# Weight splits held back by a count of VectorE's queue, and a quarter of the down projection moved between two block products

## The chip, the cores and the metric

The kernel is one program on one core of a Trainium2 chip. The metric is the device time of one execution in microseconds. Three executions of the kernel before took 2178.36, 2178.17 and 2172.22 us; the median is 2178.17 us.

## The reference, cut to what matters

Two transformer stacks run one after the other on 256 tokens of 1024 channels, all in fp32: four layers (a mixer, then a SwiGLU feed-forward), then two blocks of feed-forward, mixer, feed-forward. So there are eight feed-forward layers, four `ffn` and four `ffn_a`/`ffn_b`, all with a hidden width of 2816. The change touches only how these are scheduled, and how weights are prepared for every stage:

```python
def _swiglu(xn, w_gate, w_up, w_down):
    return (jax.nn.silu(xn @ w_gate) * (xn @ w_up)) @ w_down
...
f = _swiglu(_rms(x, g[2]), ffn_w_gate[i], ffn_w_up[i], ffn_w_down[i])
x = x + _rms(f, g[3])
```

## The kernel before, in words

**fp32 by three products.** Each fp32 operand is split into a high and a low half of type fp32r. `mm3` (line 270) multiplies high by high, high by low and low by high, three matmuls of 512 columns (lines 273, 274, 275), and then calls `tick` (line 242). One tick is thus the unit in which the program lays out its work.

**How a weight gets ready.** A weight piece of 1 MB is loaded by SyncE (line 149, in `load_step`) into one of 19 large SBUF buffers (`r8`). A unit of work is one piece, or the sum of two. `split_step` (line 189) takes the next unit in an order fixed in advance (`plan_ffn`, line 443) and splits one half of it, 128x1024: ScalarE casts it to the high half (line 220), and VectorE later subtracts to get the low half (line 184, in `flush`, which keeps one subtraction pending). If the unit is a sum, VectorE first adds the two pieces in two instructions (line 176, `pre_add`). A unit is not split further ahead than `ahead` units past the one in use, nor when `limit` units are live or fewer than two buffers are free. `need` (line 228) forces a unit's split if it has not been issued when a product wants it.

**Tasks.** Each `tick` calls `split_step` once, then steps the tasks whose time has come. A task is a generator; `spawn(gen, delay)` makes it run `delay` ticks later (at once if 0), `join` runs it on the spot. Every engine executes its instructions in the order in which the program issued them, so this order decides which instruction stands behind which.

**The feed-forward.** The hidden width is cut in chunks of 512 columns, c = 0 to 4, and one of 256. Chunks 2 and 4 (`SUMS`) are computed by `seven` (line 568), which forms the four 128x512 blocks (gate and up, for each token half) from seven block products instead of eight, in PSUM banks X, Y and Z. Each product is four ticks. Between the products stand four quarters of the down projection of the chunk before, also four ticks each: `down(c-1, h, (q,))` is token half h with weight unit q, and the unit's buffers are given back after h = 1. The order in `seven` is

- products b11 (X), b21 (Z), t1 (Y), t2 (X),
- `down(c-1,0,(0,))`, `down(c-1,1,(0,))`,
- products b22 (Y), t3 (X),
- `down(c-1,0,(1,))`, `down(c-1,1,(1,))`,
- product t4 (X).

Between products on the same bank the bank is read: X by ScalarE `copy("1")` before t2 goes on top of it, Y by `copy("5")` before b22, X by `copy("2")` before t3 (all line 587), and X by VectorE in `up1` (line 605) before t4. `gate0` (line 591) and its Silu (line 593, ScalarE) and `up0` (lines 597 and 599) are the other evacuations. The units are prepared in the order b11, b21, t1, t2, the first down unit, b22, t3, the second down unit, t4. Two `seven` in each of eight layers make 16.

Of the kernel before, what the change touches and what calls it, by code (L numbers as in the profile page):

```python
# [50 lines left out]
class Core:  # L51
    def __init__(self, ctx, tc, I, out):
        self.tc, self.nc, self.I, self.out = tc, tc.nc, I, out
        P = lambda name, **kw: ctx.enter_context(tc.tile_pool(name=name, bufs=1, **kw))
        sb = P("sb")
        self.sb = sb
        self.r8 = Slots(sb, "r8_", 19, W8, F32R)
        self.r2 = Slots(sb, "r2_", 6, 512, F32R)
        self.f2 = Slots(sb, "f2_", 10, 512, F32)
        self.gn = Slots(sb, "gn_", 2, D, F32)  # L60
        self.ps = Slots(P("ps", space=PSUM), "ps_", 8, 512, F32)
        self.dram = P("dram", space=DRAM)
        self.small_pool = sb
        self.n_small = 0
        self.later = []
        self.ticks = 0
        self.tasks = []
        self.pieces = []
        self.n_dma = self.n_split = 0
        self.sub = 0  # L70
        self.cur, self.ahead = -1, 2
        self.limit = 6
        self.live = 0
        self.raw, self.hl, self.xt = {}, {}, {}
        self.units, self.lows = [], deque()
        self.begun, self.waiting, self.n_low = set(), 0, 0
        self.uses, self.summed = [], set()
        self.z = {}
        self.raw_max = 3
        self.spare = 2  # L80
        self.reserve = 0
        self.hold = 0
        self.rr, self.nr = {}, {}
        self.pre_gains = deque()
        self.gains, self.gq = deque(), deque()
# [55 lines left out]
    def load_step(self, most=10 ** 9):  # L141
        while self.n_dma < most and self.n_dma < len(self.pieces) and len(self.r8.free) > self.spare + self.reserve and self.waiting < self.raw_max:
# [9 lines left out]
            self.waiting += 1  # L152
            self.n_dma += 1

    def used(self, i):
        self.uses[i] -= 1
        if not self.uses[i]:
            self.r8.put(self.raw.pop(i))
# [6 lines left out]
    def pre_add(self, i):  # L165

        src, first = self.units[i]
        if first is None or i in self.summed:
            return True
        if src not in self.raw or first not in self.raw or any(self.units[j][0] == src for j in range(self.n_low, i)):  # L170
            return False
        self.begin(src)
        self.begin(first)
        a, b = (self.view(self.raw[n], src) for n in (src, first))
        for sl in (slice(0, 2), slice(2, 4)):
            self.nc.vector.tensor_tensor(out=a[:, sl], in0=a[:, sl], in1=b[:, sl], op=ALU.add)  # L176
        self.used(first)
        self.summed.add(i)
        return True

    def flush(self, keep=0):
        while len(self.lows) > keep:
            lo, raw, hi, eng, i, last = self.lows.popleft()
            eng.tensor_tensor(out=lo, in0=raw, in1=hi.bitcast(F32), op=ALU.subtract)  # L184
            if last:
                self.n_low = i + 1
                self.used(self.units[i][0])

    def split_step(self, force=False, eng=None):
        i = self.n_split  # L190
        if i >= len(self.units):
            self.flush()
            return False
        src, first = self.units[i]
        if self.sub == 0:
            if first is not None and i not in self.summed:
                self.flush()
            if not force:
                for j in range(i + 1, min(i + 2, len(self.units))):
                    if self.units[j][1] is not None and j not in self.summed:  # L200
                        self.pre_add(j)
                        break
            self.load_step()
            if not force and (self.hold or i > self.cur + self.ahead or self.live >= self.limit or len(self.r8.free) < 2 + self.reserve):
                self.flush()
                self.load_step()
                return False
            if src not in self.raw or not self.pre_add(i):
                self.flush()
                return False  # L210
            if len(self.r8.free) < 2:
                self.flush()
            self.hl[i] = (self.r8.get(), self.r8.get())
            self.live += 1
            self.begin(src)
        hi, lo = (self.view(t, src) for t in self.hl[i])
        k = hi.shape[1]
        sl = slice(0, k // 2) if self.sub == 0 else slice(k // 2, k)
        raw = self.view(self.raw[src], src)[:, sl]
        self.nc.scalar.copy(out=hi[:, sl], in_=raw)  # L220
        self.lows.append((lo[:, sl], raw, hi[:, sl], eng or self.nc.vector, i, self.sub == 1))
        self.flush(1)
        self.n_split += self.sub
        self.sub ^= 1
        self.load_step()
        return True
# [52 lines left out]
    def split(self, hi, lo, src, scale=None):  # L279

        if scale is None:
            self.nc.scalar.copy(out=hi, in_=src)  # L282
            self.nc.vector.tensor_tensor(out=lo, in0=src, in1=hi.bitcast(F32), op=ALU.subtract)  # L283
        else:
            self.nc.scalar.activation(out=hi, in_=src, func=ACTF.Copy, scale=scale)
            self.nc.vector.scalar_tensor_tensor(out=lo, in0=src, scalar=scale, in1=hi.bitcast(F32), op0=ALU.mult, op1=ALU.subtract)
# [100 lines left out]
    def x_sums(self):  # L387

        tt, stt = self.nc.vector.tensor_tensor, self.nc.vector.scalar_tensor_tensor
        while len(self.r8.free) < 2:  # L390
            yield 1
        self.xs = (self.r8.get(), self.r8.get())
        self.reserve = 0
        z = self.z

        def put(j, t):
            self.split(self.xs[0][:, j * 512:(j + 1) * 512], self.xs[1][:, j * 512:(j + 1) * 512], t)

        tt(out=z[1, 1], in0=z[1, 1], in1=z[1, 0], op=ALU.subtract)
        tt(out=z[1, 0], in0=z[0, 0], in1=z[1, 0], op=ALU.subtract)  # L400
        put(0, z[1, 1])
        yield 6
        stt(out=z[0, 0], in0=z[1, 1], scalar=-1.0, in1=z[0, 0], op0=ALU.mult, op1=ALU.subtract)
        put(3, z[1, 0])
        yield 6
        stt(out=z[0, 1], in0=z[0, 0], scalar=-1.0, in1=z[0, 1], op0=ALU.mult, op1=ALU.subtract)
        put(1, z[0, 0])
        yield 6
        put(2, z[0, 1])
        self.f2.put(*z.values())  # L410
        z.clear()
        yield
# [69 lines left out]
    def ffn(self, plan, half, nxt):  # L482
# [51 lines left out]
        def both(c):  # L534
# [21 lines left out]

            def up(h, b):
                nc.vector.scalar_tensor_tensor(out=s[h], in0=b, scalar=rr[h], in1=s[h], op0=ALU.mult, op1=ALU.mult)  # L558
                self.ps.put(b)
                hidden(s[h], c, h, 512, 11)  # L560
                yield

            for q, use in enumerate((gate, up)):
                half_chunk(q, use)
                for h in range(2):
                    down(c - 1, h, (q,))

        def seven(c):
# [20 lines left out]

            def gate0():  # L590
                nc.vector.tensor_tensor(out=f["1"], in0=Z, in1=f["1"], op=ALU.add)
                self.ps.put(Z)
                nc.scalar.activation(out=f["1"], in_=f["1"], func=ACTF.Silu, scale=rr[0])
                yield

            def up0():
                nc.vector.tensor_tensor(out=f["2"], in0=Y, in1=f["2"], op=ALU.add)
                self.ps.put(Y)
                nc.vector.scalar_tensor_tensor(out=f["2"], in0=f["2"], scalar=self.nr[0], in1=f["1"], op0=ALU.mult, op1=ALU.mult)
                self.f2.put(f["1"])  # L600
                hidden(f["2"], c, 0, 512, 12)
                yield

            def up1():
                nc.vector.tensor_tensor(out=f["5"], in0=X, in1=f["5"], op=ALU.add)  # L605
                yield

            def gate1():
                g = self.f2.get()
                nc.scalar.activation(out=g, in_=X, func=ACTF.Silu, scale=rr[1])  # L610
                self.ps.put(X)
                nc.vector.scalar_tensor_tensor(out=f["5"], in0=f["5"], scalar=self.nr[1], in1=g, op0=ALU.mult, op1=ALU.mult)
                self.f2.put(g)
                hidden(f["5"], c, 1, 512, 12)
                yield
# [9 lines left out]
            product(X, "t2", "s2")  # L625
            e4 = self.spawn(copy("2", X), 2)
            down(c - 1, 0, (0,))
            down(c - 1, 1, (0,))
            self.join(e2, e3)
            product(Y, "b22", "s4")  # L630
            self.join(e4)
            e5 = self.spawn(up0(), 2)
            product(X, "t3", "s3")
            e6 = self.spawn(up1(), 1)
            down(c - 1, 0, (1,))
            down(c - 1, 1, (1,))
            self.join(e5, e6)
# [1074 lines left out]
```

## Time and profile before

| what | value |
|---|---|
| median of three executions | 2178.17 us |
| the profiled execution: time / span | 2174.96 / 2172.8 us |
| TensorE (PE) busy | 2108.3 us, 97% of the span |
| VectorE (DVE) busy | 1562.1 us, 72% |
| ScalarE (ACT) busy | 1210.7 us, 56% |
| mean granted TensorE clock | 0.995 of full speed |

The span runs from the first to the last instruction. A busy share is an average over all stages; what a change in one stage can bring is read from the idle time of PE in that stage and from what ended it.

### The profile page before, as it was taken

The page shows a single profiled execution, that of the slowest core. Times are in us where ns is not written, and L with a number is a line of the kernel's source. Part 1 is how long each engine was busy: PE and PEld are TensorE (multiplying, and loading weights), DVE is VectorE, ACT ScalarE, POOL GpSimd, SP SyncE. Part 2 cuts the span into 40 slices and gives each one's busy share as a digit, 9 for nine tenths or more (in the row PEclk, how much of TensorE's full clock was granted, in tenths as well). Part 3 has the DMA queues.
Part 4 walks back from the last instruction along what each step waited for, and adds up shares of the span by engine and source line. Part 5 has one row for each costly group of instructions (what it writes and reads, how often), then busy time and mean ns, then how long its engine had stood idle before and what let it go on. Part 6 is the DMA issues. An engine that isn't in the chain of part 4 may idle for free. (4 is left out here: it accounts for less than half of the span.)

```text
span 2172.8 us, 25010 instructions
## 1 busy us (share of the span) xinstructions
PE 2108.3 (97%) x9653; PEld 1691.3 (78%) x9653; DVE 1562.1 (72%) x2016; ACT 1210.7 (56%) x1742; POOL 77.9 (4%) x130
## 2 busy tenths in 40 slices
PE   9999989999999999999999999999999999999998
PEld 6877767777888778887788777878778787787786
DVE  6677668876577776688767765787778776479774
ACT  5555446555665555555555546774556545667543
POOL 1000000000010000000000002010000001000000
PEclk9999999999999999999999999999999999999999
DMA  8546454646444555545554564345554545344442
GB/s 294 194 162 228 150 184 143 225 156 204 157 139 174 200 198 179 194 165 194 184 193 144 171 221 164 123 142 175 201 210 168 201 151 203 123 168 163 166 155 97
DMA packets 175622, 383.74 MB, mean 177 GB/s; under 512 B 10428, under 2 KB 29116, under 8 KB 175504
## 3 DMA queue, kind: packets, MB, share of 16 engines
q1 hardware_dynamic: 172592, 372.04, 49.4%
q0 software_dynamic: 2624, 9.58, 1.3%
q8 instruction: 76, 1.25, 0.2%
q10 hardware_dynamic: 288, 0.52, 0.1%
q14 instruction: 42, 0.34, 0.0%
HBM read 380.28 MB, written 1.84 MB: 176 GB/s over the span
## 5 line engine op out<-in xcount | busy, mean ns | idle before, releaser
L273 PE MATMUL ps<-r,r 128*128 128x512 f32 (+2 forms) x2752 | 1109.0, 403 | 44.7 <-DVE f L605 37.5
L274 PE MATMUL ps<-r,r 128*128 128x512 f32 (+2 forms) x2752 | 1083.9, 394 | 4.9 <-DVE r L184 3.4
L275 PE MATMUL ps<-r,r 128*128 128x512 f32 (+2 forms) x2752 | 1085.5, 394 | 0.5 <-DVE r L283 0.3
L184 DVE TENSOR_TENSOR r<-r,r 128x1024 fp32r<-128x1024 f32 (+1 forms) x797 | 935.8, 1217 | 200.9 <-ACT r L220 197.4
L220 ACT CAST r<-r 128x1024 fp32r<-128x1024 f32 x798 | 791.7, 1043 | 412.7 <-DVE r L176 185.9
L273 PEld LDWEIGHTS ps<-r,r 128*128 128x128 f32 (+1 forms) x2752 | 518.0, 188 | 171.1 <-DVE f L605 44.4
L275 PEld LDWEIGHTS ps<-r,r 128*128 128x128 f32 (+1 forms) x2752 | 516.8, 188 | 127.0 <-DVE r L283 7.3
L274 PEld LDWEIGHTS ps<-r,r 128*128 128x128 f32 (+1 forms) x2752 | 518.0, 188 | 119.7 <-DVE r L184 8.3
L176 DVE TENSOR_TENSOR r<-r,r 128x1024 f32<-128x1024 f32 x128 | 150.9, 1220 | 54.1 <-DMA r<-in_ffn_w_up_dram 27.6
L282 ACT CAST r<-ps 128x512 fp32r<-128x512 f32 (+1 forms) x108 | 59.9, 555 | 169.0 <-PE ps L498 160.7
L283 DVE TENSOR_TENSOR r<-ps,r 128x512 fp32r<-128x512 f32 (+1 forms) x108 | 69.6, 648 | 104.3 <-ACT r L282 104.3
L558 DVE SCALAR_TENSOR_TENSOR f<-ps,rr,f 128x512 f32<-128x512 f32 x32 | 23.9, 748 | 71.8 <-PE ps L275 71.8
L302 POOL TENSOR_TENSOR st<-st,c_mhalf 128x1 f32<-128x1 f32 x28 | 16.0, 570 | 1600.2 <-DVE st L301 1599.8
L282 ACT CAST r<-f 128x512 fp32r<-128x512 f32 x84 | 51.5, 619 | 37.9 <-DVE f L366 22.1
L306 ACT ACTIVATE c_junk<-x 128x512 bf16<-128x512 f32 x56 | 35.3, 631 | 54.6 <-DVE x L339 53.7
L283 DVE TENSOR_TENSOR r<-f,r 128x512 fp32r<-128x512 f32 x84 | 57.5, 709 | 3.6 <-ACT r L282 1.5
L498 PEld LDWEIGHTS ps<-c_ident,f 128*128 128x128 f32 x352 | 45.7, 144 | 13.6 <-issue 0.8
L498 PE MATMUL ps<-c_ident,f 128*128 128x128 f32 x352 | 55.7, 278 | 0.0
L366 DVE TENSOR_TENSOR f<-ps,c_pre 128x512 f32<-128x512 f32 x52 | 33.7, 687 | 23.1 <-PE ps L292 22.5
L339 DVE SCALAR_TENSOR_TENSOR x<-f,st,x 128x512 f32<-128x512 f32 x56 | 39.6, 749 | 2.6 <-POOL st L302 0.9
L331 DVE TENSOR_TENSOR f<-ps,gn 128x512 f32<-128x512 f32 x52 | 35.5, 683 | 6.1 <-ACT c_junk L306 6.1
L530 DVE SCALAR_TENSOR_TENSOR f<-ps,rr,f 128x512 f32<-128x512 f32 (+1 forms) x32 | 19.7, 615 | 27.4 <-ACT f L529 27.3
(193 smaller groups left out, 947.7 us busy)
## 6 DMA issues: line engine op xcount, KB each, us to landing
r<-in_ffn_w_in_dram SPq DMA_DIRECT2D x80, 1024.0 KB, 5.2
r<-in_ffn_w_down_dram SPq DMA_DIRECT2D x44, 1024.0 KB, 5.0
r<-in_ffn_w_out_dram SPq DMA_DIRECT2D x44, 1024.0 KB, 5.1
r<-in_ffn_w_gate_dram SPq DMA_DIRECT2D x40, 1024.0 KB, 5.1
r<-in_ffn_w_up_dram SPq DMA_DIRECT2D x40, 1024.0 KB, 5.2
r<-in_mix_w_in_dram SPq DMA_DIRECT2D x28, 1024.0 KB, 5.1
r<-in_conv_w_in_dram SPq DMA_DIRECT2D x22, 1024.0 KB, 5.5
r<-in_attn_w_qkv_dram SPq DMA_DIRECT2D x12, 1024.0 KB, 5.4
```

What stands on the lines that cost most here:

```text
L176: self.nc.vector.tensor_tensor(out=a[:, sl], in0=a[:, sl], in1=b[:, sl], op=ALU.add)
L184: eng.tensor_tensor(out=lo, in0=raw, in1=hi.bitcast(F32), op=ALU.subtract)
L220: self.nc.scalar.copy(out=hi[:, sl], in_=raw)
L273: mm(out=out, lhsT=x[0], rhs=w[0], start=first, stop=False, skip_group_check=more)
L274: mm(out=out, lhsT=x[0], rhs=w[1], start=False, stop=False, skip_group_check=more)
L275: mm(out=out, lhsT=x[1], rhs=w[0], start=False, stop=last, skip_group_check=more)
L282: self.nc.scalar.copy(out=hi, in_=src)
L283: self.nc.vector.tensor_tensor(out=lo, in0=src, in1=hi.bitcast(F32), op=ALU.subtract)
L306: self.nc.scalar.activation(out=self.junk[:, 0:src.shape[-1]], in_=src, func=ACTF.Square, scale=scale, accum_out=acc)
L331: mul = lambda n: nc.vector.tensor_tensor(out=mg[n], in0=src[n], in1=g[:, n * 512:(n + 1) * 512], op=ALU.mult)
L339: nc.vector.scalar_tensor_tensor(out=xs, in0=mg[n], scalar=r, in1=xs, op0=ALU.mult, op1=ALU.add)
L498: nc.tensor.transpose(out=b[:, j * 128:(j + 1) * 128], in_=s[:, j * 128:(j + 1) * 128], identity=self.ident)
```

## The change

It has two parts. A count, `vector_until`, notes in ticks until when VectorE would be occupied by what has been issued: each noted instruction of `cols` columns adds (cols + 60)/640 ticks. `split_step`, unless forced, returns at once, before it loads, adds, casts or flushes anything, while the count is more than 1.5 ticks ahead. And in `seven`, `down(c-1,1,(0,))` moves from before b22 to after t3, and `up1` is spawned with no delay, so that it is issued straight behind t3 instead of one tick into the next quarter. The count is noted at lines 176, 184, 283, 399 to 406, 558, 591, 597, 599, 605 and 612; the diff is cut to three of these.

```diff
+        self.vector_until = 0.0
...
+    def vector(self, cols):
+
+        self.vector_until = max(self.vector_until, self.ticks) + (cols + 60) / 640
+
...
             self.nc.vector.tensor_tensor(out=a[:, sl], in0=a[:, sl], in1=b[:, sl], op=ALU.add)
+            self.vector(1024)
...
             eng.tensor_tensor(out=lo, in0=raw, in1=hi.bitcast(F32), op=ALU.subtract)
+            self.vector(1024)
...
             self.flush()
+            return False
+        if not force and self.vector_until > self.ticks + 1.5:
             return False
         src, first = self.units[i]
...
                 nc.vector.tensor_tensor(out=f["5"], in0=X, in1=f["5"], op=ALU.add)
+                self.vector(512)
                 yield
...
             down(c - 1, 0, (0,))
-            down(c - 1, 1, (0,))
             self.join(e2, e3)
             product(Y, "b22", "s4")
             self.join(e4)
             e5 = self.spawn(up0(), 2)
             product(X, "t3", "s3")
-            e6 = self.spawn(up1(), 1)
+            e6 = self.spawn(up1(), 0)
+            down(c - 1, 1, (0,))
             down(c - 1, 0, (1,))
             down(c - 1, 1, (1,))
             self.join(e5, e6)
```

## Rows read from the trace of the kernel before

**Rows 1.** The page, busy time of each engine.
```profile
PE 2108.3 (97%) x9653; PEld 1691.3 (78%) x9653; DVE 1562.1 (72%) x2016; ACT 1210.7 (56%) x1742; POOL 77.9 (4%) x130
```
**Rows 2.** Waits of PE: line waited for, us in total, times, longest.
```profile
PE ps L273 <- DVE f L605: 37.5, 16, 7.2
...
PE ps L273 <- ACT f L587: 2.6, 2, 2.3
```
**Rows 3.** Timeline, one `seven`, PE: start us, us, [idle before <-releaser].
```profile
781.35 0.19 PEld L273 LDWEIGHTS ps<-r,r 128*128 128x128 f32 x1 [0.50 <-ACT f L587]
...
792.66 0.50 PE L273 MATMUL ps<-r,r 128*128 128x512 f32 x1 [2.65 <-DVE f L605]
```
**Rows 4.** Timeline, the same `seven`, ScalarE.
```profile
772.27 0.72 ACT L593 ACTIVATE f<-f,rr 128x512 f32<-128x512 f32 x1 [2.78 <-DVE f L591]
774.54 2.95 ACT L220 CAST r<-r 128x1024 fp32r<-128x1024 f32 x3 [1.54 <-DVE r L176]
777.39 0.58 ACT L587 COPY f<-ps 128x512 f32<-128x512 f32 x1
777.87 2.95 ACT L220 CAST r<-r 128x1024 fp32r<-128x1024 f32 x3
780.72 0.58 ACT L587 COPY f<-ps 128x512 f32<-128x512 f32 x1
...
787.17 2.00 ACT L220 CAST r<-r 128x1024 fp32r<-128x1024 f32 x2 [1.98 <-DMA r<-in_ffn_w_up_dram]
```
**Rows 5.** Timeline, the same `seven`, VectorE.
```profile
768.16 3.48 DVE L184 TENSOR_TENSOR r<-r,r 128x1024 fp32r<-128x1024 f32 x3
771.56 0.68 DVE L591 TENSOR_TENSOR f<-ps,f 128x512 f32<-128x512 f32 x1
772.16 2.35 DVE L176 TENSOR_TENSOR r<-r,r 128x1024 f32<-128x1024 f32 x2
774.43 8.21 DVE L184 TENSOR_TENSOR r<-r,r 128x1024 fp32r<-128x1024 f32 x7
...
788.25 1.23 DVE L184 TENSOR_TENSOR r<-r,r 128x1024 fp32r<-128x1024 f32 x1 [1.61 <-ACT r L220]
789.40 0.68 DVE L597 TENSOR_TENSOR f<-ps,f 128x512 f32<-128x512 f32 x1
...
790.79 1.22 DVE L184 TENSOR_TENSOR r<-r,r 128x1024 fp32r<-128x1024 f32 x1
791.92 0.69 DVE L605 TENSOR_TENSOR f<-ps,f 128x512 f32<-128x512 f32 x1
```
**Rows 6.** The chain that ended last: start us, us from one matmul to the next.
```profile
2142.57 0.23 PE ps L273
```
**Rows 7.** Groups by line: busy us, mean ns of one | idle before.
```profile
L274 PE MATMUL ps<-r,r 128*128 128x512 f32 (+2 forms) x2752 | 1083.9, 394 | 4.9 <-DVE r L184 3.4
```
**Rows 8.** Timeline, PE: the first matmul of t4 in three other `seven`.
```profile
274.92 0.80 PE L273 MATMUL ps<-r,r 128*128 128x512 f32 x1 [7.18 <-DVE f L605]
...
1011.16 0.50 PE L273 MATMUL ps<-r,r 128*128 128x512 f32 x1 [2.32 <-DVE f L605]
...
1271.99 0.79 PE L273 MATMUL ps<-r,r 128*128 128x512 f32 x1 [2.57 <-DVE f L605]
```
**Rows 9.** Windows: us, busy of PE, PEld, DVE, ACT, POOL, clock, DMA, GB/s.
```profile
274.90:278.65 3.75, 3.73 (x11) 3.06 (x12) 2.23 (x2) 0.00 (x0) 0.00 (x0) 0.50 0.88 280
794.07:797.48 3.41, 3.41 (x12) 2.75 (x11) 3.12 (x4) 2.28 (x3) 0.00 (x0) 0.50 1.00 362
1012.50:1015.90 3.40, 3.40 (x12) 2.73 (x11) 3.40 (x4) 1.06 (x2) 0.00 (x0) 0.50 0.96 355
1271.93:1275.30 3.37, 3.31 (x9) 2.62 (x10) 2.74 (x4) 1.61 (x3) 0.00 (x0) 0.50 0.83 270
```
**Rows 10.** DMA issues: KB each, median us from issue to landing.
```profile
r<-in_ffn_w_down_dram SPq DMA_DIRECT2D x44, 1024.0 KB, 5.0
```

More of the change, by code (lines that the diff above doesn't have):

```diff
@@ L400, in x_sums @@
         tt(out=z[1, 0], in0=z[0, 0], in1=z[1, 0], op=ALU.subtract)
+        self.vector(1024)
         put(0, z[1, 1])
@@ L403, in x_sums @@
         stt(out=z[0, 0], in0=z[1, 1], scalar=-1.0, in1=z[0, 0], op0=ALU.mult, op1=ALU.subtract)
+        self.vector(512)
         put(3, z[1, 0])
@@ L406, in x_sums @@
         stt(out=z[0, 1], in0=z[0, 0], scalar=-1.0, in1=z[0, 1], op0=ALU.mult, op1=ALU.subtract)
+        self.vector(512)
         put(1, z[0, 0])
@@ L558, in up @@
                 nc.vector.scalar_tensor_tensor(out=s[h], in0=b, scalar=rr[h], in1=s[h], op0=ALU.mult, op1=ALU.mult)
+                self.vector(512)
                 self.ps.put(b)
@@ L591, in gate0 @@
                 nc.vector.tensor_tensor(out=f["1"], in0=Z, in1=f["1"], op=ALU.add)
+                self.vector(512)
                 self.ps.put(Z)
@@ L597, in up0 @@
                 nc.vector.tensor_tensor(out=f["2"], in0=Y, in1=f["2"], op=ALU.add)
+                self.vector(512)
                 self.ps.put(Y)
                 nc.vector.scalar_tensor_tensor(out=f["2"], in0=f["2"], scalar=self.nr[0], in1=f["1"], op0=ALU.mult, op1=ALU.mult)
+                self.vector(512)
                 self.f2.put(f["1"])
@@ L605, in up1 @@
                 nc.vector.tensor_tensor(out=f["5"], in0=X, in1=f["5"], op=ALU.add)
+                self.vector(512)
                 yield
@@ L612, in gate1 @@
                 nc.vector.scalar_tensor_tensor(out=f["5"], in0=f["5"], scalar=self.nr[1], in1=g, op0=ALU.mult, op1=ALU.mult)
+                self.vector(512)
                 self.f2.put(g)
```

## The prediction, made before the change was run

> **What bounds the kernel now.** I read the busy shares first: TensorE is busy in 97% of the span, VectorE in 72%, ScalarE in 56% [rows 1]. The reader is to see that some 64 us without a matmul are all that scheduling can win. Next the list of what PE waited for [rows 2]: 37.5 of these 64 us are one wait, 16 times, once in each `seven`: t4's first matmul waits for line 605, `up1`, which reads bank X. The copies' wait named beside it is 2.6 us, twice.
>
> Why is `up1` late? The timelines of one `seven` tell [rows 3 to 5]. A matmul follows the last in 0.23 us [rows 6], so a tick of three is 0.70 us. t3 starts at 781.35 and ends 2.8 us later, at 784.15; X could be read from then on. Two quarters of the down projection (5.6 us) cover the read, to 789.75; t4 starts at 792.66. VectorE reads X only at 791.92. Just ahead of it stand `up0` and two low halves of weights, and the first of these, at 788.25, came after an idle 1.61 us for a cast that itself waited for a load [rows 4, 5]. These weights are wanted only after t4. So VectorE is not short of speed here: its queue holds work for later, issued early, in front of work for now.
>
> ScalarE shows the same. `copy("5")` may run when t1 ends (8 + 4 ticks after the first product starts; with t3 at tick 28 = 781.35, tick 0 is 761.75 and this is 770.15), but runs at 777.39, behind three casts that waited for VectorE's adds; `copy("2")` at 780.72 stands behind three more [rows 4].
>
> **What the stall costs.** The profile's 37.5 us count idle from a matmul's modelled end, 0.39 us after its start [rows 7], where the next could start after 0.23. Each stall therefore hides 0.16 us more: 37.5 + 16 x 0.16 = 40 us. There is a second price. After the wait in this `seven` and in three others [rows 3, 8] a stretch is granted half clock, 1.2 instead of 2.4 GHz, for 3.41, 3.75, 3.40 and 3.37 us [rows 9]; PE stood idle before all four, and I read the idle time as the reason. At half speed half of the time is lost: 13.9 / 2 = 7 us. I take both as gone if the wait goes: 47 us.
>
> **The moved quarter.** It is 12 matmuls, four ticks, 2.8 us. It issues no load, but its end returns a down unit's two buffers eight ticks (5.6 us) later. Behind t3, cover for `up1` grows from 8 to 12 ticks, 8.4 us. In front of b22 cover shrinks by 2.8 us: b22 would start at 775.75 and t3 at 778.55 without waits. With the queues as they are, `copy("5")` ends at 777.97, b22 waits 2.2 us and ends at 780.8, and t3 waits 0.5 us more for `copy("2")`, done at 781.30. So the move alone would lose 16 x 2.7 = 43 us of the 47. Everything hangs on what the hold does to the two queues.
>
> **The hold.** A low half is noted as 1084/640 = 1.69 ticks, 1.18 us. The trace has three in 3.48 and seven in 8.21 us, 1.16 to 1.17 each [rows 5], so the count runs true while VectorE waits for nothing. I counted this `seven` by hand under the new rule, in ticks from its first product, with the buffers that become free: a cast adds nothing, its low half is noted with the next cast, and a step goes only if the count is at most 1.5 past the tick. The count stands at 9.7 after the evacuation at tick 4; b22's casts are held to ticks 9 and 10 and its low halves end at 11.7 and 14.3 with `gate0` (12.6) between them; t3's casts go at 13 and 14, its first low half ends at 16.0; the two adds of t4 and t3's second low half end at 21.1; then nothing is issued until tick 20. The second down unit and t4 follow at 20 to 25; `up0` (26) ends at 29.6 and `up1` (28) at 30.5.
>
> - b22 starts at tick 20: its weights are 5.7 ticks early. `copy("5")` is issued at 14 behind t3's two casts alone (2.00 us by the pair in rows 4): Silu to about 13.6, casts to 16.6, copy to 17.4. In time by 2.6 ticks, 1.8 us.
> - t3 starts at 24 and wants its second half at 26: 8 and 4.9 ticks early (3.4 us for the nearer). `copy("2")` is issued at 18 behind one cast: done by 20, 4 ticks early.
> - t4 starts at 40: `up1` is done 9.5 ticks, 6.6 us, before. Ahead of it stand only low halves of t4 and the down unit; the first of a later unit, and so the one whose load was late, comes behind it, at tick 30.
>
> So the evacuations' wait goes and the weights still arrive. Total work on each engine is unchanged. VectorE's later work moves into the chunk behind, where `both` wants 12 low halves in 48 ticks. A load is issued with the hold up to four ticks later, but its start is set by the buffer: the second down piece is asked for at tick 9, lands 5.0 us (7 ticks) later [rows 10], and is wanted at tick 32. Elsewhere one unit alone never trips the hold (1.69 - 1 = 0.69, then 3.39 - 2 = 1.39 ticks ahead), and units are issued several ticks before their product, so I cost the hold outside `seven` at nothing; each that came late would cost up to a low half, 1.2 us [rows 5].
>
> What I charge: the wait of b22 or t3 for a copy, seen twice before [rows 2], has less room in the first `seven`, where loads start late. Bounds are nothing and 43 us (above); nearest is the count's margin of 1.8 us, so I take 0.2 us for each of the 16, 3 us. Sum: 2174.96 - 47 + 3 = 2131 against the profiled execution's time. That execution lies 3.2 us below the median shown, so I forecast between the two, **2133 us**; its own range is 2124 to 2144.
>
> **A rule against it.** t4's gap comes back in all 16, 2.3 us in the mean [rows 2]. The Trainium skill (Perfetto Trace Analysis, "Optimization Strategy") says that a gap repeating on the engine that should be saturated can mean that SBUF has too few buffers for the next tile. By that rule holding two buffers 5.6 us longer makes it worse; the trace agrees in part, since a load was waited for. It is the second rival below, and is priced there from rows.
>
> **The rivals.**
>
> - *The waits move to the copies.* If other casts stay ahead of `copy("5")` and `copy("2")`, or the hold does not bite before tick 14, PE waits 2.7 us a `seven` in place of t4's: 2175 - 47 + 43 = 2171, no change to speak of. For it: three casts stand in front of each copy now. Against: the count leaves two and one. Decides: `copy("5")` later than tick 20. Chance 0.08.
> - *Buffers, and loads with them.* If the units behind t4 get in front of `up1` again, or the later buffers delay what `down` wants next, each `seven` keeps about the 1.6 us that VectorE idled for a cast [rows 5]: 16 x 1.6 = 26 us, and half of the clock's 7 with it: 2131 + 29 = 2160. Against: the count puts these low halves two ticks behind `up1`. Chance 0.12.
> - *Held too long (slower).* If the hold keeps t3's unit back until its product asks, `need` forces it: two adds, a cast and a low half before the first matmul, 2 x 1.17 + 1.0 + 1.22 = 4.6 us [rows 4, 5], 16 times 74: 2175 - 47 + 74 = 2202. It decides where t3's second low half ends over 5 ticks later than counted, and is slower than before from 47/16 = 2.9 us beyond that. For it: held steps also flush and load nothing. Against: 3.4 us of room, and a count that matches the rows. Chance 0.06.
> - Forecast 0.74.
>
> **How the numbers follow.** What a measurement of this kernel can tell from no change is about 0.3%, 6.5 us. Faster: the forecast and the second rival, and a quarter of the first, 0.88. Same: most of the first, 0.06. Slower: 0.06. The range reaches from all named waits gone (2131 - 3 - 3.4 - 2.6 = 2122; the 3.4 is what lines 274 waited for low halves, rows 7) up to the second rival, 2160; outside are the first and the third, 0.14, and some misses.
>
> **What would show it.** In the profile after: PE's wait for `up1` near nothing; `up1` right behind t3, with about five low halves between t4's adds and `up0`, where rows 5 show eight and more; fewer than three casts before each copy; half-clock stretches behind t4 gone; no new line of PE waiting over 5 us. I am wrong if line 587 or 184 takes the place of the wait, or if forced splits appear in `seven`.

## The result, and the profile after

The changed kernel takes 2119.04 us (median; 2118.69 to 2120.63), the kernel before 2178.24 us beside it. The ratio is 0.9736 with a 95% interval of 0.9719 to 0.9754: 2.6% faster. The direction is as forecast, but the time lies 14 us under the 2133 forecast, 5 us under the forecast's own range (from 2124) and 3 us under the lower end of the wide one (2122). The profiled execution took 2119.03 us, 55.9 less than that of before, with a span of 2116.5 and a mean granted clock of 0.999 (0.995 before).

The page's busy times answer to [rows 1]; the number of instructions is the same, and PE's share rises to 99%:

```profile
PE 2090.4 (99%) x9653; PEld 1688.8 (80%) x9653; DVE 1559.2 (74%) x2016; ACT 1211.7 (57%) x1742; POOL 76.9 (4%) x130
```

Of the 56 us gained, PE's idle time is 38 (span less busy: 64.5 before, 26.1 after) and its busy time the other 18. The prediction's sentence that the 64 us without a matmul are all that scheduling can win was thus no bound: busy time holds delays too, as shown below.

The waits of PE answer to [rows 2]. `up1` (now line 622) is in the list no more; the costliest of what is left is a tenth of it, and for a copy (now line 601) PE waits once. The third line, the low half of the hidden tile (the product of gate and up that `down` multiplies), has grown from 0.3 us:

```profile
PE ps L283 <- DVE r L190: 3.9, 7, 1.3
PE ps L302 <- DVE x L349: 3.7, 3, 2.0
PE ps L284 <- DVE r L292: 3.0, 4, 1.2
...
PE ps L282 <- ACT f L601: 1.1, 1, 1.1
```

The timelines of the same `seven`, ScalarE and VectorE, answer to [rows 4, 5]. Here b22 starts at 754.50, t3 at 757.30 and t4 at 768.88:

```profile
750.41 2.00 ACT L229 CAST r<-r 128x1024 fp32r<-128x1024 f32 x2 [0.40 <-DVE r L190]
752.32 0.58 ACT L601 COPY f<-ps 128x512 f32<-128x512 f32 x1
752.79 1.05 ACT L229 CAST r<-r 128x1024 fp32r<-128x1024 f32 x1
753.75 0.58 ACT L601 COPY f<-ps 128x512 f32<-128x512 f32 x1
```

```profile
752.64 2.35 DVE L181 TENSOR_TENSOR r<-r,r 128x1024 f32<-128x1024 f32 x2
754.91 5.76 DVE L190 TENSOR_TENSOR r<-r,r 128x1024 fp32r<-128x1024 f32 x5
760.59 0.69 DVE L612 TENSOR_TENSOR f<-ps,f 128x512 f32<-128x512 f32 x1
761.31 0.75 DVE L615 SCALAR_TENSOR_TENSOR f<-f,rr,f 128x512 f32<-128x512 f32 x1
761.98 0.68 DVE L622 TENSOR_TENSOR f<-ps,f 128x512 f32<-128x512 f32 x1
```

Two casts and one cast stand in front of the copies where there were three and three, and five low halves stand between t4's adds and `up0` where rows 5 show eight and more. The copies end 1.6 and 3.0 us before their product, `up1` 6.2 us before t4.

### The profile page after: what moved, and what is told of

Read it like the earlier page. It is cut to its first block, busy times and chain, and to the rows that moved or that the text cites. A ratio compares the mean times of both kernels' runs of the same rounds, so it can differ in the third digit from the quotient of the medians.

```text
span 2116.5 us, 24989 instructions
## 1 busy us (share of the span) xinstructions
PE 2090.4 (99%) x9653; PEld 1688.8 (80%) x9653; DVE 1559.2 (74%) x2016; ACT 1211.7 (57%) x1742; POOL 76.9 (4%) x130
## 5 line engine op out<-in xcount | busy, mean ns | idle before, releaser
L316 ACT ACTIVATE c_junk<-ps 128x512 bf16<-128x512 f32 x52 | 31.0, 597 | 17.0 <-PE ps L284 16.2
```

Of the source, the lines that this page charges most:

```text
L316: self.nc.scalar.activation(out=self.junk[:, 0:src.shape[-1]], in_=src, func=ACTF.Square, scale=scale, accum_out=acc)
```

## The experiments

All of them stand beside runs of the kernel before on the same chip. Runs 1 to 4, 5 to 8, 9 to 12 and 13 to 16 are four groups, each on a chip of its own; only the groups of runs 5 and 13 have the change itself beside the others, so elsewhere a difference of a few us to the change is less sure. Line numbers of the variants differ by a few.

| run | median us | ratio to before | 95% interval |
|---|---|---|---|
| the change | 2119.04 | 0.9736 | 0.9719 to 0.9754 |
| 1 move alone | 2175.56 | 1.0000 | 0.9984 to 1.0015 |
| 2 hold alone | 2124.43 | 0.9767 | 0.9743 to 0.9792 |
| 3 hold in `seven` only | 2123.33 | 0.9767 | 0.9742 to 0.9791 |
| 4 `up1` late | 2168.27 | 0.9972 | 0.9955 to 0.9988 |
| 5 the change again | 2119.59 | 0.9748 | 0.9727 to 0.9769 |
| 6 hold, `up1` at once | 2124.16 | 0.9766 | 0.9748 to 0.9783 |
| 7 quiet before `up1` | 2156.81 | 0.9918 | 0.9893 to 0.9943 |
| 8 count a third larger | 2393.84 | 1.1007 | 1.0974 to 1.1040 |
| 9 hold up to b22 | 2161.37 | 0.9938 | 0.9919 to 0.9957 |
| 10 limit 3.0 | 2120.61 | 0.9750 | 0.9734 to 0.9766 |
| 11 limit 0.7 | 2116.82 | 0.9731 | 0.9716 to 0.9746 |
| 12 count a quarter larger | 2127.19 | 0.9779 | 0.9763 to 0.9794 |
| 13 the change, a third time | 2118.68 | 0.9747 | 0.9732 to 0.9761 |
| 14 hold alone again | 2123.31 | 0.9770 | 0.9755 to 0.9785 |
| 15 limit 0.7 again | 2115.85 | 0.9736 | 0.9722 to 0.9751 |
| 16 hold alone, limit 0.7 | 2116.82 | 0.9739 | 0.9722 to 0.9757 |

**1. The move without the hold.**

```diff
-        if not force and self.vector_until > self.ticks + 1.5:
+        if not force and self.vector_until > self.ticks + 1e9:
```

> The quarter moved and up1 undelayed, but no hold (the limit of 1.5 ticks is set out of reach). Theory (the prediction's): without the hold the copies still run behind three casts each, so b22 and t3 wait 2.7 us a seven in place of up1: 16 x 2.7 = 43 us given back of the 47, about 2171 us, and PE's waits name line 587's copy (line 601 here) with some 30 to 45 us. Rival: the move itself brings most of the gain, since cover for up1 grows by 2.8 us where the stall was 2.3: 2125 to 2140 us, and the copies' wait stays under 10 us.

Measured 2175.56 us, no change. The list of PE's waits names the copies:

```profile
PE ps L282 <- ACT f L601: 42.1, 26, 5.3
```

ScalarE's timeline shows them where [rows 4] had them, behind three casts each:

```profile
773.15 2.94 ACT L229 CAST r<-r 128x1024 fp32r<-128x1024 f32 x3 [1.54 <-DVE r L181]
776.00 0.57 ACT L601 COPY f<-ps 128x512 f32<-128x512 f32 x1
776.47 2.95 ACT L229 CAST r<-r 128x1024 fp32r<-128x1024 f32 x3
779.32 0.58 ACT L601 COPY f<-ps 128x512 f32<-128x512 f32 x1
```

The wait for `up1` is gone and an equal one has taken its place, 42.1 us of idle time where 43 were worked out (46 by the starts of matmuls, the measure of the table further down). The moved quarter alone brings nothing.

**2. The hold without the move.**

```diff
             down(c - 1, 0, (0,))
+            down(c - 1, 1, (0,))
             self.join(e2, e3)
...
-            e6 = self.spawn(up1(), 0)
-            down(c - 1, 1, (0,))
+            e6 = self.spawn(up1(), 1)
```

> The hold with the old order of quarters and up1 one tick late as before. Theory: the order of VectorE's queue is what made up1 late, so the hold alone takes the 16 waits away: up1 is issued at tick 33 with a count of about 35.6 against t4 at 40, and both copies have 2.8 us more room than after the change: 2115 to 2125 us, no wait for up1 over 3 us in total. Rival: cover of 12 ticks is needed, and up1 still waits behind two low halves of later units (issued at ticks 29 and 30): 0.7 to 1.6 us a seven remain, 2130 to 2145 us.

Measured 2124.43 us, within the theory's range: nearly all of the gain comes from the hold. Of the waits for `up1` one of 0.3 us is left.

**3. The hold inside `seven` only.**

```diff
-        if not force and self.vector_until > self.ticks + 1.5:
+        if not force and self.in_seven and self.vector_until > self.ticks + 1.5:
...
                 self.join(self.st)
+                self.in_seven = True
                 seven(c)
+                self.in_seven = False
```

> The change, with the hold in force only inside seven; everywhere else splits are issued as before the change. Theory (the hold outside seven costs and brings nothing): 2116 to 2122 us, the same as the change within 0.2%. Rival: part of the 12 us beyond the forecast comes from the hold in other stages: 2125 to 2131 us.

Measured 2123.33 us, between the two: its runs (2122.41 to 2126.36) lie 1.6 to 7.7 us over those of the change (2118.69 to 2120.78 in the result and run 5), so the hold elsewhere brings perhaps 4 us. In its list of PE's waits the low half of the hidden tile stands with 6.5 us in 8 waits, against 3.0 in 4 after the change. It was not run beside the change, and the intervals against before overlap: a hint, not more.

**4. `up1` put back late.**

```diff
-            e6 = self.spawn(up1(), 0)
+            e6 = self.spawn(up1(), 99)
```

`join` then issues it just ahead of t4.

> The change, with up1 issued only right before t4, behind a low half of a later unit; copies and weights keep the order of the change. This puts back the one wait and nothing else. Theory: PE waits for up1 about 2.0 to 2.5 us in each seven, 32 to 40 us, and half-clock stretches come back behind some of these waits (0 to 7 us): 2150 to 2166 us. What it falls short of the kernel before (2178) is then the part of the gain that is not up1: the copies and their like, some 10 us. Rival: all of the gain hangs on up1 and the clock: 2170 to 2180 us.

Measured 2168.27 us, above the theory's range by 2 us and under the rival's. PE waits again, and the mean granted clock is back at 0.994 in the profiled execution (0.990 to 0.995 over all ten; before beside it 0.989 to 0.997):

```profile
PE ps L282 <- DVE f L622: 39.5, 16, 3.7
```

```profile
core 0: 2164.6 us, clock 0.994
```

This one wait with its clock is worth about 2168.3 - 2119.3 = 49 us, where 2119.3 is the mean of the result and run 5. The other 8 us of the gain (2176.1 - 2168.3; 2.6 to 9.8 by the interval) are something else.

**5 and 6. The change again, and the hold with `up1` undelayed in the old order.** Run 6 is run 2 with `spawn(up1(), 0)`.

> The changed kernel once more, beside the three others of this call. Both theories: 2117 to 2122 us.

> The hold, the old order of the quarters, and up1 issued without delay right behind t3. Theory: with the hold up1 is in time anyway, so this tick is worth nothing: the same as the hold alone, 2121 to 2126 us, and what is left to the change (2119) is what the moved quarter brings by issuing up0 four ticks earlier, and with it the transposes of the hidden tile whose low half PE waited for 5.8 us with the hold alone and 3.0 us after the change. Rival: the missing tick of up1 is the difference, 2117 to 2120 us.

Measured 2119.59 and 2124.16 us, side by side, with runs that do not overlap (2119.15 to 2120.78, 2122.24 to 2124.84). Issuing `up1` one tick earlier is worth nothing that shows (2124.16 with it, 2124.43 without it in run 2); the rival falls.

**7. Quiet from b22 to `up1`, no count.** The kernel before with this:

```diff
+        if not force and self.quiet:
+            return False
         src, first = self.units[i]
...
             self.join(e2, e3)
+            self.quiet = True
             product(Y, "b22", "s4")
...
                 nc.vector.tensor_tensor(out=f["5"], in0=X, in1=f["5"], op=ALU.add)
+                self.quiet = False
```

> The kernel before (no count, quarters in the old order, up1 one tick late) with one thing added: from b22 on no split is issued until up1 is issued. So the casts of the units behind t4, and their low halves, go behind up1; the queue up to b22 is as long as before. Theory: these few low halves, with the load they wait for, are the whole stall: up1 runs 3 us or more before t4, 40 us and 7 us of clock come back, the copies' small waits stay (2 to 6 us): 2124 to 2132 us. Rival: the long queue that VectorE carries since t1 (busy without a gap to 782.64 in the seven of rows 5) still makes up1 late: a stall of 0.5 to 1.5 us stays in most, 2140 to 2155 us.

Measured 2156.81 us, 2 us above the rival's range and far from the theory's. `up1` is in time and its wait is gone, as the theory says; but PE has a new one, for the high half of the hidden tile (`split`, here line 285), which `down` wants next:

```profile
PE ps L276 <- ACT r L285: 22.4, 10, 8.4
```

ScalarE's timeline shows why. The casts of later units, which now stand behind `up1`, still wait for their loads, and the hidden tile's cast stands behind them:

```profile
785.68 1.99 ACT L223 CAST r<-r 128x1024 fp32r<-128x1024 f32 x2 [0.99 <-DMA r<-in_ffn_w_up_dram]
789.38 1.99 ACT L223 CAST r<-r 128x1024 fp32r<-128x1024 f32 x2 [1.70 <-DMA r<-in_ffn_w_down_dram]
791.27 0.58 ACT L285 CAST r<-ps 128x512 fp32r<-128x512 f32 x1
```

Half clock costs this run 12 us of extra time, by the measure of the table further down, where it cost the kernel before 8. So my price for this edit was wrong: to move the late splits behind one reader hands their wait to the next.

**8 and 12. The count a third and a quarter larger.** 480 and 512 in place of 640 columns a tick.

> The change with every note a third larger (480 columns a tick in place of 640), so that the count no longer runs with VectorE but ahead of it. The third rival's case (held too long): about 125 units are then issued only when their product asks, each at about 2.3 us for cast and low half, sums 4.6 us: 290 to 450 us more than the change, 2400 to 2570 us, with PE waiting for line 190. Against it, if VectorE still has its slack and the forced splits hide behind other work: under 2200 us.

> The change with every note a quarter larger (512 columns a tick). No more forced splits than in the change beyond one unit, but units of seven are issued only 2 to 5 ticks ahead of their product, where the change has 8 and more. Theory: this is the edge on the way to the slow case: PE waits for line 190 in most seven, 0 to 1.5 us each: 2120 to 2145 us. Rival: the loss starts only where splits are forced: 2117 to 2122 us.

Measured 2393.84 us, 10% slower than before, just under what was worked out, and 2127.19 us, within the theory's range. PE's waits of the former, which make up 176 of the 275 us that it takes more than the change (some 75 us of the rest are extra time at half clock, by the measure of the table further down; the mean granted clock is 0.957):

```profile
PE ps L282 <- ACT r L229: 111.8, 54, 6.6
PE ps L283 <- DVE r L190: 64.1, 82, 2.5
```

and the first of the latter:

```profile
PE ps L283 <- DVE r L190: 13.0, 13, 3.6
```

The slow rival is real. In the change the count is at 640 columns a tick; at 512 the weights begin to come late, and at 480 the kernel falls over the edge.

**9. The hold only up to b22, in the old order.** `early` is true from the first product of `seven` to b22.

```diff
-        if not force and self.vector_until > self.ticks + 1.5:
+        if not force and self.early and self.vector_until > self.ticks + 1.5:
```

> The old order of quarters, up1 one tick late, and the hold in force only from the start of seven up to b22. From b22 on splits are issued freely, so the same two low halves of the unit behind t4 stand around up0 in front of up1 as in the kernel before. Theory as mended by the run that was quiet before up1: those low halves were late because their load was, and the load because its buffer was freed late by VectorE's long queue; with the early hold the load starts 3 us sooner, so they no longer wait and up1 is in time though it stands behind them: 2121 to 2130 us, ScalarE's waits for loads well under the 119 us of before. Rival: it is the order alone, so up1 is late again by 1 us or more in most seven: 2140 us and up.

Measured 2161.37 us: the mended theory falls, the rival's range holds. PE waits for `up1` (here line 623) again, if less, and for the hidden tile:

```profile
PE ps L283 <- DVE f L623: 20.6, 15, 3.6
PE ps L283 <- ACT r L292: 11.5, 8, 3.4
```

VectorE's timeline of the `seven` whose t4 starts at 720.35 shows that here no late load was needed for it:

```profile
707.91 9.17 DVE L191 TENSOR_TENSOR r<-r,r 128x1024 fp32r<-128x1024 f32 x8
717.00 0.68 DVE L613 TENSOR_TENSOR f<-ps,f 128x512 f32<-128x512 f32 x1
...
718.39 1.22 DVE L191 TENSOR_TENSOR r<-r,r 128x1024 fp32r<-128x1024 f32 x1
719.52 0.68 DVE L623 TENSOR_TENSOR f<-ps,f 128x512 f32<-128x512 f32 x1
```

VectorE does not stand idle ahead of `up1`; eight low halves in front of `up0` and one behind it are enough to make `up1` late. Neither a shorter queue ahead of b22 (run 9) nor a free way from b22 to `up1` (run 7) was enough; of the versions run here, those whose hold lasts through `seven` take the waits away.

**10, 11 and 13 to 16. The limit, and the moved quarter once more.** 3.0 and 0.7 ticks in place of 1.5.

> The change with 3.0 ticks in place of 1.5 as the limit of the hold. Theory: about one more half is let into each queue; up1 keeps its room, copy 5 runs a tick later but before tick 20: 2117 to 2126 us. Rival: the margin of copy 5 (2.2 ticks measured) is used up and the copies wait again: 2130 us and up.

> The change with 0.7 ticks as the limit. Theory: splits go one at a time, weights still 5 ticks early in issue: 2116 to 2124 us, the same as the change. Rival: t3's second half is late and PE waits for line 190 some 10 to 30 us: 2130 to 2150 us.

> The changed kernel, five rounds beside the next three. 2118 to 2121 us.

> The hold with the old order of quarters once more. Theory (the moved quarter adds to the hold, since up0 and with it the hidden tile's split come four ticks earlier): 4 to 5.5 us above the change, 2122 to 2126 us, with an interval that excludes no difference. Rival: the difference between calls was drift: within 1.5 us of the change.

> The limit of 0.7 ticks, beside the change. Theory (a shorter queue goes on paying, since casts are issued later and find their loads landed): 2 to 3.5 us under the change, 2115 to 2118 us. Rival: same as the change within 1 us.

> The old order of quarters with the limit of 0.7. Theory: only one low half of a later unit stands before up1 and none waits for a load; the moved quarter still brings its 4 to 5 us: 2119 to 2124 us. Rival: with the shorter queue the move is worth nothing: 2115 to 2118 us.

The limit of 3.0 measured 2120.61 us, that of 0.7 2116.82. In runs 13 to 16, side by side, the change took 2118.68 us (2118.24 to 2119.62), the hold alone 2123.31 (2122.59 to 2125.75): the moved quarter brings 4.6 us on top of the hold. The medians at 0.7 are 2115.85 us with it and 2116.82 without, runs overlapping: there it brings nothing that can be told. The median at the limit of 0.7 is 2.8 us under that of the change, but the runs only just do not touch (2115.72 to 2118.16 against 2118.24 to 2119.62); it is the lowest median here.

Where at least a part of the 4.6 us is shows in what the weight loads of PE waited for. The low half of the hidden tile, line 292, in the change, the hold alone, the limit of 0.7 and that without the move (runs 13 to 16), one line of each view:

```profile
PEld ps L284 <- DVE r L292: 9.2, 18, 1.5
```

```profile
PEld ps L284 <- DVE r L292: 15.8, 27, 1.9
```

```profile
PEld ps L284 <- DVE r L292: 4.1, 13, 0.4
```

```profile
PEld ps L284 <- DVE r L292: 4.3, 14, 0.4
```

15.8 - 9.2 = 6.6 us go with the moved quarter at 1.5, and nothing at 0.7. Not all of a weight load's wait is lost to the matmuls: in PE's own list the same wait is 2.8 and 4.9 us (runs 13 and 14). With the quarter moved `up0` is issued four ticks earlier, and the hidden tile's transposes and split with it; that the split finds VectorE free anyway with the shorter limit is my reading of the last two lines, not a test.

## Why the prediction was right, and where its size was wrong

**The bound and the stall.** Right. `up1` was late through the order of VectorE's queue, not through its speed: busy time is the same (1559.2 us after, 1562.1 before) and the wait is gone. The price was right too: the table below has 40.0 + 6.6 us for the 47 worked out from idle, pace and clock, and run 4, which puts back such a wait alone, is 49 us slower. The 7 us of the clock were for the four stretches behind `up1`, which cost 6.4; a fifth stretch at half clock in the trace before (326.44, behind another wait) and one near the start of the trace after (10.97) cost 1.7 each and cancel.

**The moved quarter.** Right: alone it loses what it gains, 42.1 us of idle time for copies against 43 (run 1).

**The hold.** Right, to within 1 us in the one `seven` compared. Counted by hand against the trace after, in us ahead of need: `copy("5")` 1.8 against 1.6, `copy("2")` 2.8 against 3.0, `up1` 6.6 against 6.2. t3's second low half, the first of the five at 754.91, leaves some 2.6 us where 3.4 were counted. That the hold is the part which makes the change is shown by runs 1 and 2; that its count must not run far ahead of VectorE, by 8 and 12.

**What I charge: the step that failed.** The sum stood at 2131 with 3 us added for copies that would come late. In the trace after, one such wait of 1.2 us is there, in the first `seven` as feared; the rest of what copies cost before is gone, and the sum had no term for it. I had read that cost as 2.6 us in two waits [rows 2]. The list of what PE's weight loads waited for shows more waits, 17 before and one after:

```profile
PEld ps L273 <- ACT f L587: 10.5, 17, 2.7
```

```profile
PEld ps L282 <- ACT f L601: 1.5, 1, 1.5
```

A matmul's modelled end lies 0.16 us behind the start of the next, so a wait shorter than that is not idle time of PE at all, and a longer one is cut by it. I had added this to `up1`'s 16 waits and to no other. Taken from the starts of successive matmuls in both traces, against the median spacing of each kind, 56.3 us of span between first and last matmul divide so:

| | before | after | gain | forecast |
|---|---|---|---|---|
| t4 waiting for `up1` | 40.0 | 0 | 40.0 | 40 |
| extra time in half-clock stretches | 8.3 | 1.7 | 6.6 | 7 |
| products waiting for a copy | 5.8 | 1.2 | 4.6 | -3 |
| single matmuls 0.05 to 0.12 us late | 30.2 | 26.2 | 4.0 | 0 |
| all other | | | 1.1 | 0 |

So the terms that I took from rows held within 1 us, and the one that I put in by judgement had the wrong sign: 7.6 of the 12 us between 44 forecast and 56 measured. Of the 5.8 us before, the two named waits are half; the other half is 15 waits too short for the list of PE. Another 4 us of gain are small delays that no row of mine showed: some 37 fewer matmuls start late, and their cause stays open. The last 2 us of the 14 are the step from the profiled execution up to the median, which the profiled pair (2174.96 and 2119.03) does not have. Executions of the kernel before go with their clock, from 2168.16 us at a mean of 0.997 to 2183.22 us at 0.989 (beside runs 1 to 4), while those of the change have 0.997 to 0.999 (result and run 5): the step up goes with a lower clock, which the change takes away. The range failed with it: its lower end was "all named waits gone", and the waits that the list of PE names are not all that PE waits.

**The second rival.** It did not come about, but run 7 is its like: where splits whose loads are late stand ahead of a reader, here the hidden tile's cast, the reader waits. By how much loads are late does not decide it: ScalarE waited 119 us for feed-forward weights before, 50 after the change, yet 120 at the limit of 3.0, which is within 2 us of the change. I read from this that it matters what stands behind the waiting cast. The rule on too few buffers (the Trainium skill, Perfetto Trace Analysis, "Optimization Strategy") names what such a gap can mean, and it was not that here: the buffers are as many, and one unit is held longer, while the repeating gap is gone.

**Left open.** What the hold brings outside `seven` (run 3 hints at 4 us); what the 4 us of small delays are; and which part of run 9's loss is the number of low halves and which the loads, since ScalarE's casts still wait for loads there.

## What to carry to other kernels

When the busiest engine waits for a short instruction on an engine that has time to spare, look at what is queued ahead of it: here work for later, issued as early as buffers allowed, cost 40 us and the clock with it. Put a bound on the queue instead of on single places: run 7 shows the wait going to the next reader, and run 1 shows more cover for one reader being taken from another. A count of the queue needs an honest rate, here within 2% of the trace; a quarter too large cost some 8 us and a third too large 275. And take what a wait costs from the starts of the next instructions, not from idle time alone: much of the gain that the forecast missed stood in no row of idle time.

## What was not expected of the hardware and its profile

Putting back 16 waits of 2.5 us in the mean brought the mean granted clock down from 0.999 to 0.994 (run 4), with PE standing idle before the stretches at 1.2 GHz. Six of the 16 waits, of 2.3 to 3.7 us idle, have such a stretch beside them, and ten do not. Taken as in the table above, 42 us of that run's time are the wait and some 10 are extra time at half clock, against 1.7 after the change. And PE's idle time in this profile is less than what a wait costs: the same 16 waits of the kernel before came out as 37.5 us by idle, 40.0 by the starts of matmuls, and 44.4 by the weight loads:

```profile
PEld ps L273 <- DVE f L605: 44.4, 16, 7.6
```
